# Splitting the sixth weight group of each expert, and the second gated half, in a hybrid attention and mixture-of-experts layer

## The chip, the cores and the metric

The kernel runs on one core of a Trainium2 chip, in one launch. The metric is the device time of one execution in microseconds (us), the median of several runs. A change of 1% is about 10 us here.

## The reference, cut to what matters

The layer is an attention and pooling block followed by a mixture of experts. Only the experts are touched by the change:

```
u: (1024 tokens, 1024)            16 experts, w_gate, w_up: 1024x512, w_down: 512x1024
top-1 group of 4, then top-2 experts inside it, softmax weights -> combine
for e in range(16):
    h = silu(u @ w_gate[e]) * (u @ w_up[e])
    y += combine[:, e] * (h @ w_down[e])
out = layer_norm(alpha * x + (1 + gate2) * y)
```

All arrays are fp32.

## The kernel before, in words

The first half of the kernel (attention, pooling, output projection, first layer norm, routing) ends a little after 540 us. From there the experts are worked through one after the other, unrolled in the program as `expert(0)` to `expert(15)`, and a final layer norm over all tokens closes the kernel.

Routing has sorted the tokens by expert. Each expert has a main block of 128 token slots, and a tail of up to 32 or 64 further tokens, which is run only where the expert has more than 128 (or 160) tokens, inside `tc.If(n_e > P)` (lines 1223 and 1242). With these inputs six experts run a tail, three of them a second one. From the third expert on, busy and less busy experts alternate.

The weights of an expert are six groups of 1 MB, `raw(0)` to `raw(5)`, each 128 partitions by 4 x 512 fp32. Groups 0 to 3 are gate and up, groups 4 and 5 are down. A ring of 11 buffers (`RAW`) holds them; SyncE's queue loads them far ahead (`refill`, `load_group`).

A product of the main block is made in one of two ways.
- Split (`mm_split`, lines 1056 to 1061): the weights are cut into a rounded high part in `HR`, copied by ScalarE (line 941), and the remainder in `LR`, subtracted by VectorE (line 944). The activations are cut the same way. Three matmuls in fp32r (a 4-byte format) then replace one fp32 product: high by high, high by low, low by high. A group is split in two halves of 128 x 1024 each (`split_group`). There are three buffers each for `HR` and `LR` (`NH = 3`), so a group's split waits until TensorE has finished with the group three places earlier; `split_ahead(s)` issues that split right behind the matmuls on group s.
- Plain fp32 (line 1176): TensorE takes the raw weights.

`NSP = 5` groups of an expert are split: the four of gate and up, and the first of down. The main block of one expert runs in this order: `gate_up(0)` (24 matmuls, columns 0 to 255 of gate and of up), `gated` (a0: Silu on ScalarE, the product on VectorE), `gate_up(1)` with `turn(a0)` inside it (two transposes of a0 on TensorE, then a copy out of PSUM; for a0 also the split, lines 1157 and 1158, into a tile `hs`), `gated` (a1), the tail's first half if there is one, `prep(e + 1)` (transposes and split of the next expert's tokens), `turn(a1)` (line 1161, a plain copy into `hh`), `down(0)` (12 split matmuls on group 4), `split_ahead`, `down(1)` (4 plain fp32 products on group 5), `emit` (two VectorE instructions out of PSUM, line 1195), `send` (an indirect DMA that adds the rows to `ybuf`), and the tail's second half.

The framework lays out the order on each engine itself, from the dependencies and its own estimate of when things are ready; each engine then works strictly in that order. In the trace the tail's second half (line 1242) lies in the middle of `down(0)`, and a0's transposes lie behind the 37th of the 48 matmuls of gate and up.

In the last expert the final layer norm of all tokens (`final`, lines 1002 to 1021) is threaded in: `tick()` counts the products and pulls one piece of it every second one. Its first instruction in a piece is ordered behind the newest ScalarE or VectorE instruction of the main path that `note` has recorded (`behind`).

Of the kernel before, what the change touches and what calls it, by code (L numbers as in the profile page):

```python
# [52 lines left out]
WS = "vvvv"  # L53
PRE = 0
SPLIT = 800
NSP = 5
RB = 0
TB = 1
MT = 2
# [33 lines left out]
def hybrid_layer(ctx: ExitStack, tc: tile.TileContext, x, c, w_ada, b_ada, w_qk, w_v, w_p, w_pool,  # L93
# [838 lines left out]
    def note(k, ins):  # L932
        newest[k] = ins
        return ins

    def split_group(s):
        m = NG * (s // NSP) + s % NSP
        r, l, h = RAW[m % NL], LR[s % NH], HR[s % NH]
        for a in range(2):
            cs = slice(2 * a, 2 * a + 2)  # L940
            rnd = note("a", nc.scalar.activation(h[:, cs], r[:, cs], AF.Copy))  # L941
            if s == 0:
                after(turned[0], rnd)
            sub = note("d", nc.vector.tensor_sub(l[:, cs], r[:, cs], h[:, cs]))  # L944
            if s < NH:
                after(ready, sub)
# [93 lines left out]
    def expert(e, n_e):  # L1040
# [10 lines left out]
        hts = []  # L1051

        def raw(g, j):
            return RAW[(NG * e + g) % NL][:, j]

        def mm_split(o, xh, xl, s, j, first, end):
            tick()
            h, l = HR[s % NH][:, j], LR[s % NH][:, j]
            nc.tensor.matmul(o, xh, h, start=first, stop=False)  # L1059
            nc.tensor.matmul(o, xh, l, start=False, stop=False)  # L1060
            nc.tensor.matmul(o, xl, h, start=False, stop=end)  # L1061

        def split_ahead(s):
            if s + NH < NE * NSP:
                split_group(s + NH)
# [22 lines left out]
        def tick():  # L1088
            ticks[0] += 1
            n = ticks[0] - BS1  # L1090
            if last and n >= 0 and n % BR1 == 0:
                next(bulk, None)

        def gate_up(half, mid=None):
            pg = ps.tile([P, 512], F32, name="mm", bufs=6)
            for k in range(KC):
                s = NSP * e + 2 * half + k // GRP
                mm_split(pg, xa_h[:, k], xa_l[:, k], s, k % GRP, k == 0, k == KC - 1)
# [52 lines left out]
        def turn(s):  # L1151
            pt = ps.tile([P, 2, P], F32, name="tr")
            for j in range(2):
                nc.tensor.transpose(pt[:, j], s[:, j * P:(j + 1) * P], ident)
            if not hts:
                hh = act.tile([P, 2, 2, P], F32R, name="hs")
                note("a", nc.scalar.activation(hh[:, 0], pt, AF.Copy))
                note("d", nc.vector.tensor_sub(hh[:, 1], pt, hh[:, 0]))
            else:
                hh = act.tile([P, 2, P], F32, name="hh", bufs=4)  # L1160
                note("a", nc.scalar.activation(hh, pt, AF.Copy))
            hts.append(hh)
# [3 lines left out]
        def down(g):  # L1166
            for dh in range(2):
                if g == 0:
                    pys.append(ps.tile([P, 512], F32, name="mm", bufs=6))
                for f in range(2):  # L1170
                    k, w = 2 * g + f, raw(4 + g, 2 * f + dh)
                    if g < NSP - 4:
                        mm_split(pys[dh], hts[g][:, 0, f], hts[g][:, 1, f], NSP * e + 4 + g, 2 * f + dh, k == 0, k == 3)
                    else:
                        tick()
                        nc.tensor.matmul(pys[dh], hts[g][:, f], w, start=k == 0, stop=k == 3)
# [41 lines left out]
        pa0 = gate_up(0)  # L1218
        a0 = gated(pa0)
        pa1 = gate_up(1, {MT: lambda: turn(a0)})  # L1220
        a1 = gated(pa1)
        t = {}
# [8 lines left out]
        if not last:  # L1231
            prep(e + 1)
        turn(a1)
        down(0)
        split_ahead(NSP * e + 4)
        down(1)
        ys_[1] = ytail
        for _ in bulk if last else ():
            pass
# [24 lines left out]
    for e in range(NE):  # L1264
        src = cnt[0:1, e:e + 1] if e < NS else cntp[0:1, e - NS:e - NS + 1]
        n_e = nc.values_load(src, min_val=0, max_val=S)
        if e == 0:
            scratch = act.tile([P, D], F32, name="y", bufs=1)[0:1, :2 * ND * ND].rearrange("p (r a b) -> p r a b", r=2, a=ND)
            for r, (o, v) in enumerate(((perm, eidx[0:1, NS:]), (cntp, cntf[:, NS:]))):
                calc = by_place(o, v, scratch[:, r])  # L1270
                after(ready, next(calc))
                next(calc, None)
        expert(e, n_e)
# [45 lines left out]
    with tc.If(top > P + HB):  # L1319
# [8 lines left out]
        e = nc.values_load(perm[0:1, ND - 1:ND], min_val=0, max_val=NE - 1)  # L1328
# [63 lines left out]
```

## Time and profile before

| | |
|---|---|
| Median of 3 runs | 1014.16 us (1008.32 to 1016.25) |
| Profiled execution, its own time | 1010.06 us |
| Its span, first to last instruction | 1008.3 us |
| Mean granted TensorE clock | 0.928 |
| Busy: TensorE, VectorE, ScalarE, GpSimd | 84%, 66%, 48%, 38% of the span |

The profile calls TensorE's matmuls PE and its weight loads PEld, VectorE DVE, ScalarE ACT, GpSimd POOL and SyncE's DMA queue SP. Times in a timeline count from the start of the span. The busy shares are means over stages with different limits; what the change is worth is read from the experts' stretch, about 557 to 957 us.

### The profile page before, as it was taken

How to read it: one execution, taken by the hardware profiler on the slowest of the kernel's cores; microseconds unless marked ns; L12 is line 12 of the kernel's file. 1: busy time of each engine (PE TensorE's matmuls, PEld its weight loads, DVE VectorE, ACT ScalarE, POOL GpSimd, SP SyncE). 2: the span in 40 equal slices, each digit the busy share in tenths (PEclk: the TensorE clock that was granted, in tenths of full speed). 3: DMA queues.
4: the chain of work that ended last, by engine and by line, in shares of the span. 5: the costliest groups of instructions: out<-in, count | busy, mean ns of one | idle time of the engine just before them, and what ended most of it. 6: DMA issues, size and time to landing. Idle time of an engine off the chain costs nothing. (4 is left out here: it accounts for less than half of the span.)

```text
span 1008.3 us, 14528 instructions
## 1 busy us (share of the span) xinstructions
PE 849.4 (84%) x4983; PEld 611.6 (61%) x4984; DVE 661.5 (66%) x990; ACT 487.3 (48%) x794; POOL 380.9 (38%) x337
## 2 busy tenths in 40 slices
PE   4979897999999888989882889999999999998820
PEld 3658675777767666766651666665666666666500
DVE  7889787374355656868486765657666575757553
ACT  3341453554454655444423555546555565656450
POOL 4685082060041335664554421212222222222383
PEclk7899998999999998988995989999999999999965
DMA  8937741010010342112647487778787888888731
GB/s 306 316 133 226 257 143 59 22 43 25 27 40 1 110 162 84 64 63 85 230 131 284 157 306 251 247 282 272 292 304 288 296 294 293 291 295 300 253 136 64
DMA packets 42488, 187.24 MB, mean 186 GB/s; under 512 B 7921, under 2 KB 8977, under 8 KB 30096
## 3 DMA queue, kind: packets, MB, share of 16 engines
q1 hardware_dynamic: 34608, 168.57, 45.5%
q0 software_dynamic: 7776, 17.33, 7.0%
q8 instruction: 61, 1.00, 0.4%
q14 instruction: 43, 0.35, 0.1%
HBM read 169.19 MB, written 25.33 MB: 193 GB/s over the span
## 5 line engine op out<-in xcount | busy, mean ns | idle before, releaser
L376 DVE TENSOR_TENSOR_SCAN N<-N,zcol 128x1023 f32<-128x1023 f32 (+7 forms) x64 | 88.9, 1426 | 86.5 <-ACT N L369 86.5
L1059 PE MATMUL mm<-HR,xa 128*128 128x512 f32 x256 | 106.6, 416 | 0.1
L1060 PE MATMUL mm<-LR,xa 128*128 128x512 f32 x256 | 101.3, 396 | 0.0
L961 POOL DMA_INDIRECT V<-u2d,TP x28 | 35.0, 1250 | 172.8 <-PEq L1223 65.5
L944 DVE TENSOR_TENSOR LR<-raw,HR 128x1024 fp32r<-128x1024 f32 x70 | 85.2, 1223 | 22.9 <-ACT HR L941 19.1
L1061 PE MATMUL mm<-HR,xa 128*128 128x512 f32 x256 | 99.8, 391 | 0.0
L941 ACT ACTIVATE HR<-raw 128x1024 fp32r<-128x1024 f32 x70 | 74.0, 1060 | 41.1 <-PE mm L1061 40.6
L944 DVE TENSOR_TENSOR LR<-mixT,HR 128x1024 fp32r<-128x1024 f32 x62 | 75.5, 1223 | 19.9 <-ACT HR L941 16.7
L941 ACT ACTIVATE HR<-mixT 128x1024 fp32r<-128x1024 f32 x62 | 65.3, 1058 | 37.4 <-PE mm L1061 37.3
L392 ACT ACTIVATE AT<-tr 128x512 f32<-128x512 f32 (+3 forms) x96 | 42.6, 487 | 51.6 <-PE tr L391 51.5
L446 PE MATMUL mm<-uh,wh 128*128 128x512 f32 x160 | 66.5, 416 | 0.2 <-ACT mixT L436 0.2
L448 PE MATMUL mm<-uh,wl 128*128 128x512 f32 x160 | 64.7, 404 | 0.0
L447 PE MATMUL mm<-ul,wh 128*128 128x512 f32 x160 | 64.5, 403 | 0.0
L419 POOL TENSOR_TENSOR mixT<-pT 128x344 f32<-128x344 f32 (+1 forms) x12 | 16.3, 1367 | 127.7 <-ACT pT L407 127.7
L391 PE MATMUL tr<-ident,arena 128*128 128x128 f32 x288 | 46.4, 299 | 18.0 <-ACT AT L392 9.2
L396 PE MATMUL mm<-AT,V 128*64 128x128 f32 x576 | 55.1, 302 | 3.9 <-ACT AT L392 3.1
L1059 PEld LDWEIGHTS mm<-HR,xa 128*128 128x128 f32 x256 | 48.3, 189 | 13.9 <-issue 4.1
L1060 PEld LDWEIGHTS mm<-LR,xa 128*128 128x128 f32 x256 | 48.4, 189 | 12.7 <-issue 3.6
L1061 PEld LDWEIGHTS mm<-HR,xa 128*128 128x128 f32 x256 | 48.1, 188 | 9.7
L391 PEld LDWEIGHTS tr<-ident,arena 128*128 128x128 f32 x288 | 36.8, 155 | 27.9 <-ACT AT L392 13.7
L378 DVE TENSOR_TENSOR arena<-arena,N 128x1023 f32<-128x1023 f32 (+7 forms) x64 | 53.6, 869 | 0.0
L649 PE MATMUL mm<-wol,mh 128*128 128x512 f32 x128 | 51.4, 401 | 2.2 <-POOL wol L533 1.7
(352 smaller groups left out, 2100.5 us busy)
## 6 DMA issues: line engine op xcount, KB each, us to landing
raw<-in_w_moe_dram SPq DMA_DIRECT2D x42, 1024.0 KB, 9.1
mixT<-in_w_moe_dram SPq DMA_DIRECT2D x36, 1024.0 KB, 10.1
arena<-in_w_moe_dram SPq DMA_DIRECT2D x18, 1024.0 KB, 9.8
arena<-in_w_ada_dram SPq DMA_DIRECT2D x24, 512.0 KB, 4.4
wada<-in_w_ada_dram SPq DMA_DIRECT2D x12, 512.0 KB, 6.1
mixT<-in_w_ada_dram SPq DMA_DIRECT2D x12, 512.0 KB, 4.1
ybuf<-sg SPq DMA_DIRECT2D x8, 512.0 KB, 2.6
wraw<-in_w_qk_dram SPq DMA_DIRECT2D x6, 512.0 KB, 3.4
```

Of the source, the lines that this page charges most:

```text
L376: nc.vector.tensor_tensor_scan(N[:, hd, 1:nk], N[:, hd, 1:nk], zcol.to_broadcast([P, nk - 1]), 1.0, op0=OP.mult, op1=OP.add)
L378: nc.vector.tensor_mul(E[:, hd, 1:nk], E[:, hd, 1:nk], N[:, hd, 1:nk])
L391: nc.tensor.transpose(pt[:, j], E[:, hd, (g + j) * P:(g + j + 1) * P], ident)
L396: mm = nc.tensor.matmul(po[h * HD:(h + 1) * HD, :P], V[:, cp, i + j, h * HD:(h + 1) * HD], ATs[h][j // 4][:, j % 4], start=j == 0, stop=j ...
L446: nc.tensor.matmul(po, h[:, k], uh[:, k, cs], start=k == 0, stop=False)
L447: nc.tensor.matmul(po, h[:, k], ul[:, k, cs], start=False, stop=False)
L448: nc.tensor.matmul(po, l[:, k], uh[:, k, cs], start=False, stop=k == KC - 1)
L941: rnd = note("a", nc.scalar.activation(h[:, cs], r[:, cs], AF.Copy))
L944: sub = note("d", nc.vector.tensor_sub(l[:, cs], r[:, cs], h[:, cs]))
L1059: nc.tensor.matmul(o, xh, h, start=first, stop=False)
L1060: nc.tensor.matmul(o, xh, l, start=False, stop=False)
L1061: nc.tensor.matmul(o, xl, h, start=False, stop=end)
```

## The change

`NSP` goes from 5 to 6, so that group 5 (the second of down) is split like the others, and `down(1)` uses `mm_split` instead of the plain product. `turn(a1)` makes the same split tile as `turn(a0)`. A `split_ahead` is added behind `down(1)`. The number of split buffers stays at three.

```
-NSP = 5
+NSP = 6
...
-            if not hts:
+            if len(hts) < NSP - 4:
                 hh = act.tile([P, 2, 2, P], F32R, name="hs")
                 note("a", nc.scalar.activation(hh[:, 0], pt, AF.Copy))
                 note("d", nc.vector.tensor_sub(hh[:, 1], pt, hh[:, 0]))
...
         split_ahead(NSP * e + 4)
         down(1)
+        split_ahead(NSP * e + 5)
         ys_[1] = ytail
```

## Rows read from the trace of the kernel before

**Rows 1.** The page: busy us, share of the span and instructions of each engine.
```profile
PE 849.4 (84%) x4983; PEld 611.6 (61%) x4984; DVE 661.5 (66%) x990; ACT 487.3 (48%) x794; POOL 380.9 (38%) x337
```
**Rows 2.** Windows: PE, PEld, DVE, ACT, POOL busy (instructions), clock, DMA share, GB/s.
```profile
817.00:846.00 29.00, 26.46 (x187) 17.66 (x186) 15.71 (x18) 15.75 (x24) 3.73 (x4) 1.00 0.82 303
846.00:866.50 20.50, 19.11 (x81) 13.67 (x80) 17.43 (x20) 12.90 (x16) 8.58 (x5) 1.00 0.82 279
```
**Rows 3.** Waits of the experts' stretch: total us, times, longest.
```profile
ACT HR L941 <- PE mm L1061: 87.5, 115, 5.2
```
**Rows 4.** Groups by shape from 440 us on: busy us, mean ns, idle before, releaser.
```profile
L1059 PE MATMUL mm<-HR,xa 128*128 128x512 f32 x256 | 106.6, 416 | 0.1
L944 DVE TENSOR_TENSOR LR<-raw,HR 128x1024 fp32r<-128x1024 f32 x70 | 85.2, 1223 | 22.9 <-ACT HR L941 19.1 <-DVEq L1223 0.2
...
L941 ACT ACTIVATE HR<-raw 128x1024 fp32r<-128x1024 f32 x70 | 74.0, 1060 | 41.1 <-PE mm L1061 40.6 <-ACTq L1223 0.2
...
L1176 PE MATMUL mm<-raw,hh 128*128 128x512 f32 x56 | 27.1, 628 | 0.0
...
L1158 DVE TENSOR_TENSOR hs<-tr,hs 128x256 fp32r<-128x256 f32 x16 | 6.7, 419 | 1.0 <-ACT hs L1157 1.0
...
L981 ACT ACTIVATE xb<-tr 128x256 f32<-128x256 f32 x12 | 3.9, 381 | 1.4 <-PE tr L980 1.4
```
**Rows 5.** Timeline of PE, end of an expert with one tail, and the next.
```profile
843.04 3.59 PE L1176 MATMUL mm<-raw,hh 128*128 128x512 f32 x8
...
846.71 0.39 PE L1060 MATMUL mm<-LR,xa 128*128 128x512 f32 x1
...
851.73 0.39 PE L1061 MATMUL mm<-HR,xa 128*128 128x512 f32 x1
...
854.91 0.39 PE L1154 MATMUL tr<-ident,silu 128*128 128x128 f32 x2
```
**Rows 6.** Timeline of DVE over the same stretch.
```profile
843.88 1.21 DVE L1137 TENSOR_TENSOR ytail<-ytail,sg 32x1024 f32<-32x1024 f32 x1 [6.20 <-ACT ytail L1136]
845.02 2.34 DVE L944 TENSOR_TENSOR LR<-mixT,HR 128x1024 fp32r<-128x1024 f32 x2
847.29 1.39 DVE L1195 SCALAR_TENSOR_TENSOR y<-mm,TP,sg 128x512 f32<-128x512 f32 x2
849.15 1.23 DVE L944 TENSOR_TENSOR LR<-mixT,HR 128x1024 fp32r<-128x1024 f32 x1 [0.47 <-ACT HR L941]
...
854.40 0.41 DVE L1148 TENSOR_TENSOR silu<-silu,mm 128x256 f32<-128x256 f32 x1
```
**Rows 7.** Timeline of DVE, end of the expert without a tail that follows.
```profile
863.75 2.36 DVE L944 TENSOR_TENSOR LR<-raw,HR 128x1024 fp32r<-128x1024 f32 x2 [1.72 <-ACT HR L941]
...
869.66 1.23 DVE L944 TENSOR_TENSOR LR<-raw,HR 128x1024 fp32r<-128x1024 f32 x1 [1.73 <-ACT HR L941]
```
**Rows 8.** Timeline of DVE, first subtraction of an expert behind two tails.
```profile
799.82 1.23 DVE L944 TENSOR_TENSOR LR<-mixT,HR 128x1024 fp32r<-128x1024 f32 x1 [0.22 <-ACT HR L941]
```
**Rows 9.** Timeline of PE: its waits at the tail's branch in two experts.
```profile
594.41 1.94 PE L971 MATMUL tr<-ident,V 128*128 128x128 f32 x8 [3.73 <-PEq L1223]
...
859.08 0.47 PE L1059 MATMUL mm<-HR,hs 128*128 128x512 f32 x1 [1.24 <-PEq L1223]
```
**Rows 10.** Windows around that longer wait, columns as in rows 2.
```profile
592.00:596.00 4.00, 1.59 (x8) 1.62 (x9) 1.35 (x2) 0.51 (x2) 1.00 (x1) 0.60 0.23 49
```
**Rows 11.** Timeline of DVE, then POOL, in the last expert and the final norm.
```profile
948.92 1.53 DVE L998 BATCH_NORM_STATS2 bn<-raw 128x6 f32<-128x512 f32 x2 [1.66 <-DMA raw<-ybuf]
...
953.79 1.29 DVE L998 BATCH_NORM_STATS2 bn<-raw 128x6 f32<-128x512 f32 x2 [3.09 <-DMA raw<-ybuf]
...
982.98 0.74 DVE L1195 SCALAR_TENSOR_TENSOR y<-mm,TP,sg 128x512 f32<-128x512 f32 x1
...
955.61 0.83 POOL L1008 TENSOR_SCALAR mod<-mod 128x1 f32<-128x1 f32 x1 [1.18 <-DVE mod L1000]
```

More of the change, by code (lines that the diff above doesn't have):

```diff
@@ L55 @@
 SPLIT = 800
-NSP = 5
+NSP = 6
 RB = 0
@@ L1154, in turn @@
                 nc.tensor.transpose(pt[:, j], s[:, j * P:(j + 1) * P], ident)
-            if not hts:
+            if len(hts) < NSP - 4:
                 hh = act.tile([P, 2, 2, P], F32R, name="hs")
@@ L1236, in expert @@
         down(1)
+        split_ahead(NSP * e + 5)
         ys_[1] = ytail
```

## The prediction

> **What bounds the kernel now.** The page comes first [rows 1]: TensorE is busy 84% of the span, VectorE 66%. The change lies in the experts alone, so the next view is the windows of one pair of experts, one with a tail and the one without that follows it [rows 2]. In both TensorE is busy over 90% of the time at the full clock of 2.4 GHz (granted 1.00), but VectorE is not the same in the two: 15.71 of 29.00 us with a tail, 17.43 of 20.50 us without. The waits [rows 3] say who leads: ScalarE's rounding copies waited 87.5 us for TensorE to give a split buffer back, and no DMA stands there, so the weights land in time and TensorE sets the pace. The timelines of the pair [rows 5 to 7] then show how far behind TensorE the other two are when each piece is wanted, and the last expert's timeline [rows 11] which part of the end hangs on what.
>
> **What TensorE saves.** The four plain products of `down(1)` are eight records. They start at 843.04; the next expert's second matmul starts at 846.71, and its first took one step before that. A step is read from the split matmuls: 22 of them from 846.71 to 851.73 make 0.228 us each [rows 5]. So plain fp32 holds TensorE for 846.71 - 0.228 - 843.04 = 3.44 us, and the twelve split matmuls will hold it for 12 x 0.228 = 2.74 us: 0.70 us less per expert. I take the step between starts, not the durations, which overlap. The Trainium skill, in "Perfetto Trace Analysis", section "Identifying the Most-Contended Engine", says that matmul busy time is no measure, because matmuls are pipelined. By the durations [rows 4] the eight records would cost 8 x 0.628 = 5.02 us and the twelve 12 x 0.416 = 4.99 us, and the saving would be nothing; the trace sides with the rule, since twelve durations of 0.416 us do not fit into the time between starts.
>
> The saving counts in experts 0 to 14: 15 x 0.70 = 10.5 us. In the last expert it does not: its own rows leave PSUM at 982.98 [rows 11], behind the final norm's work on VectorE, long after its matmuls.
>
> **What it adds.** Per expert two ScalarE copies of 1.06 us, two subtractions of 1.22 us, and the low half of a1, 0.42 us, on VectorE [rows 4]. Two subtractions in a row take 2.34 us [rows 6], which is the figure used below.
> - ScalarE: the new copies stand behind the last matmuls of `down(1)`. ScalarE does 12.90 us of work in 20.50 [rows 2] and waits there for TensorE; 15.0 in 19.8 still fits. Nothing.
> - a1's low half: VectorE waits 1.72 us just there in an expert without a tail [rows 7], 6.20 us with one [rows 6]. Nothing; without that cover 0.42 us.
> - SyncE: group 5's buffer now comes free when it has been split, during `gate_up(1)`, and not behind `down(1)`. The loads queued behind it go out earlier. Since no wait is for weights [rows 3], nothing. The splits of the next expert's groups 0, 1 and 2 each move one group later. The tightest is group 2: its subtractions would be done at 851.0 (below), and TensorE asks for it 24 steps, 5.47 us, after its start at 845.78, at 851.25; the second half is asked for later still. In time, with little left.
> - VectorE's extra pair behind an expert without a tail: 2.34 us of work and a start that comes 0.70 us earlier, against 1.73 us of idle time [rows 7], leaves it 1.3 us late; the y instructions ahead of it wait for `down(1)` and so also move by up to 0.7, which leaves 0.6. From there to a0's multiply the four subtractions come at TensorE's pace, 854.40 - 849.15 = 5.25 us, where they could take 2 x 2.34 = 4.68 [rows 6]: 0.57 us is made up. Nothing is left; at most 0.7 us in each of nine such experts, 6.3 us.
> - VectorE's extra pair behind a tail. Here the queue is fuller: the tail's own multiply at 843.88, the pair for the next expert, the two y instructions up to 847.29 + 1.39 = 848.68 [rows 6]. With the new pair behind them VectorE is free at 848.68 + 2.34 = 851.02. TensorE's next expert starts at 843.04 + 2.74 = 845.78 and not 846.48, so the first subtraction of that expert, now 849.15 - 846.48 = 2.67 us behind the start, is wanted at 848.45. VectorE is 2.57 us late; 0.57 is made up, and a0's multiply comes 2.0 us late. And a0's multiply has no slack: it ends at 854.40 + 0.41 = 854.81 [rows 6], and a0's transposes start at 854.91 [rows 5], in the middle of TensorE's stream, with the next matmuls queued behind them in order. Behind two tails VectorE's idle time was 0.22 and not 0.47 us [rows 6, 8], so 2.25 us late. Six experts have a tail, since the copies of line 981 come twice in each and there are twelve [rows 4].
>
> The price of this last point is open between 0 and 3 x 2.0 + 3 x 2.25 = 12.75 us. Nothing, if the new order on TensorE puts later work where it would wait; all of it, if the order stays. The order is laid out anew for the changed program, and transposes that start 0.10 us behind the multiply's end look like an order that counts VectorE's time. Then they move back, and VectorE meets TensorE again at a1's multiply, another four subtractions and 0.57 us later: 2.0 - 0.57 = 1.4 us late, in a chain (multiply, transposes, copy, subtraction, `down(1)`) that has only `down(0)`'s 2.74 us to hide behind and hid there exactly before. I take 1.4 us, six times: 8.4 us.
>
> **The end.** The final norm starts from the landing of expert 14's rows, so it moves with TensorE's sum. In the last expert one more pair is subtracted, ahead of the norm's first statistics at 948.92, which waited 1.66 us for a DMA [rows 11]; that covers it. The second statistics at 953.79 were free of the main path. Now the newest recorded VectorE instruction there is a1's low half, behind Silu, multiply, transposes and copy, and the statistics are ordered behind it. GpSimd waits for them at 955.61 and is busy from then on. Estimate from these rows: a1's low half at about 955.3, so 1.5 us late; between 0 and 1.6. I take 1.5, as GpSimd's wait is plain.
>
> Sum: -10.5 + 8.4 + 1.5 = -0.6 us. On the profiled execution's 1010.06 us that gives 1009.5. It lies 4.1 us under the median of the runs; on the median the forecast is 1013.5 us, no measurable change. Its own range is -6 to +5 us, for a stall of 0.5 to 2.2 us behind a tail.
>
> **The rivals.**
> - VectorE's lateness is hidden and the whole saving arrives. For it: VectorE has 13 us to spare in an expert with a tail [rows 2], so what is late must only be carried there, by an order that puts a0's and a1's transposes far enough back. Against it: the chain of a1 has little to hide behind. 1014.16 - 10.5 = 1003.7 us.
> - Slower: the stalls cost TensorE its clock. In the trace TensorE once waited 3.73 us at a branch [rows 9], and the granted clock of the window around it fell to 0.60 [rows 10], between its two levels of 1.2 and 2.4 GHz; a wait of 1.24 us [rows 9] left it at 1.00 [rows 2]. The new stalls of 2.0 to 2.25 us lie between. From wherever between those two waits the clock falls, each costs another 40% of 4 us, 1.6 us. With the order unchanged: -10.5 + 12.75 + 1.5 + 6 x 1.6 = +13.4 us, 1027.5 us. Against it: matmuls stand close on both sides of each stall.
> - The change does not act as written: the new order moves the tail's branch or the evacuations elsewhere, and the time moves for reasons outside this sum, by a few us either way. The 3.73 us wait, whose cause the rows do not show, could go or come again.
>
> **How the numbers follow.** 0.55 for the forecast, 0.25 for the hidden lateness, 0.12 for the clock, 0.08 for the rest. 1% is about what a measurement of this kernel tells from no change. Faster by more than that needs all of the saving and something more, or an end without its 1.5 us: 0.18. Slower by more: the clock, and the upper end of the costs (12.75 + 6.3 + 1.6 - 10.5 = +10.2): 0.15. Within 1%: 0.67. The range takes in the hidden case and the upper end of the costs, 1002.5 to 1023 us, and leaves out the clock.
>
> **What would show it.** Starts of one expert's `down(1)` and of the next expert 2.74 us apart, 0.70 less than before. VectorE without idle time from the tail's multiply through the first subtractions of the next expert. A new wait of TensorE on VectorE at line 1154, at a0 or a1, in the six experts that follow a tail, and none in the others. Granted clock 1.00 there. If no such wait stands there, the lateness was hidden; if TensorE waits for a subtraction of line 944 instead, group 2 came too late, and the price is larger than I set it.

## The result, and the profile after

The changed kernel takes 1039.63 us (median of 4 runs, 1038.15 to 1041.72), the kernel before 1011.88 us on the same chip (4 runs, 1008.32 to 1016.25): 1.0274 times as long, 95% interval 1.0224 to 1.0324. That is slower by 2.7%, and outside the predicted range. The profiled execution took 1041.72 us, its span is 1039.9 us.

The page's first line, as in [rows 1], shows more of the same work and no engine that became the bound:

```profile
PE 852.0 (82%) x5047; PEld 630.9 (61%) x5048; DVE 697.1 (67%) x1038; ACT 518.9 (50%) x826; POOL 446.1 (43%) x337
```

Where the time went is read from the starts of the experts (the first split matmul of each). From the first start to that of the last expert it is 379.7 us in the trace before, 409.9 after: 30.2 of the 31.6 us by which the span grew arise among the experts. Windows over just these stretches, first the trace before, then after (columns as in [rows 2]):

```profile
557.46:937.18 379.72, 350.81 (x2131) 241.62 (x2131) 251.91 (x280) 218.87 (x308) 96.01 (x72) 0.98 0.79 279
```
```profile
557.30:967.20 409.90, 352.71 (x2191) 258.85 (x2191) 282.92 (x323) 246.71 (x337) 161.47 (x72) 0.96 0.72 259
```

TensorE's busy time grew by 1.9 us, its idle time from 28.9 to 57.2 us: it waits. GpSimd is busy 65 us longer with the same 72 instructions, and the clock is granted at 0.96 instead of 0.98. The waits say what TensorE waits for, and what VectorE waits for (total, times, longest). The first line, TensorE at a0's transposes, and the second, VectorE at the landing of y, are not there at all among the experts before; the third answers to [rows 3], and over the same stretch, up to the start of the last expert, it was 83.1 us before: ScalarE waits less for TensorE, which leads by less.

```profile
PE tr L1154 <- DVE silu L1148: 25.8, 11, 3.0
```
```profile
DVE y L1195 <- DMA ybuf<-y,TP: 14.0, 4, 4.2
...
ACT HR L941 <- PE mm L1061: 64.2, 101, 5.4
```

The pair of experts of [rows 2], 28.85 and 20.50 us before, starts at 833.73, 866.15 and 888.74 after; the third window is the next expert with a tail:

```profile
833.73:866.15 32.42, 27.17 (x191) 19.37 (x190) 17.39 (x21) 17.47 (x27) 5.79 (x4) 0.95 0.77 284
866.15:888.74 22.59, 18.92 (x85) 14.37 (x84) 20.06 (x23) 15.06 (x19) 16.85 (x4) 1.00 0.71 255
888.74:920.47 31.73, 26.12 (x191) 18.24 (x190) 17.16 (x21) 17.47 (x27) 5.92 (x4) 1.00 0.79 285
```

Both kinds of experts are slower. VectorE's timeline behind the tail, the counterpart of [rows 6]:

```profile
865.12 1.22 DVE L1137 TENSOR_TENSOR ytail<-ytail,sg 32x1024 f32<-32x1024 f32 x1 [5.87 <-ACT ytail L1136]
866.26 2.34 DVE L944 TENSOR_TENSOR LR<-arena,HR 128x1024 fp32r<-128x1024 f32 x2
868.53 0.73 DVE L1195 SCALAR_TENSOR_TENSOR y<-mm,TP,sg 128x512 f32<-128x512 f32 x1
869.19 2.34 DVE L944 TENSOR_TENSOR LR<-mixT,HR 128x1024 fp32r<-128x1024 f32 x2
871.46 0.73 DVE L1195 SCALAR_TENSOR_TENSOR y<-mm,TP,sg 128x512 f32<-128x512 f32 x1
872.12 4.61 DVE L944 TENSOR_TENSOR LR<-mixT,HR 128x1024 fp32r<-128x1024 f32 x4
876.66 0.40 DVE L1148 TENSOR_TENSOR silu<-silu,mm 128x256 f32<-128x256 f32 x1
876.99 1.21 DVE L944 TENSOR_TENSOR LR<-mixT,HR 128x1024 fp32r<-128x1024 f32 x1
```

No brackets behind the first line: VectorE never idles from the tail's multiply to a0's. Between the two stand four pairs of subtractions instead of three, and TensorE, which has to have a0's product for its transposes, stands still (its timeline, counterpart of [rows 5]):

```profile
874.76 0.39 PE L1061 MATMUL mm<-HR,xa 128*128 128x512 f32 x1
877.12 0.44 PE L1154 MATMUL tr<-ident,silu 128*128 128x128 f32 x2 [1.97 <-DVE silu L1148]
```

Now GpSimd behind a tail, first the trace before, then after; then VectorE and TensorE in the expert after it. Here is what the prediction had not looked at:

```profile
845.88 2.85 POOL L1205 DMA_INDIRECT ybuf<-ytail,TP  x1 [7.87 <-ACT HR L941]
```
```profile
867.11 12.44 POOL L1205 DMA_INDIRECT ybuf<-ytail,TP  x1 [8.32 <-ACT HR L941]
879.86 2.39 POOL L1205 DMA_INDIRECT ybuf<-y,TP  x1 [0.30 <-PEq L1223]
```
```profile
892.94 0.75 DVE L1195 SCALAR_TENSOR_TENSOR y<-mm,TP,sg 128x512 f32<-128x512 f32 x1 [4.04 <-DMA ybuf<-y,TP]
893.61 2.39 DVE L944 TENSOR_TENSOR LR<-raw,HR 128x1024 fp32r<-128x1024 f32 x2
895.93 0.74 DVE L1195 SCALAR_TENSOR_TENSOR y<-mm,TP,sg 128x512 f32<-128x512 f32 x1
896.59 4.61 DVE L944 TENSOR_TENSOR LR<-raw,HR 128x1024 fp32r<-128x1024 f32 x4
901.13 0.40 DVE L1148 TENSOR_TENSOR silu<-silu,mm 128x256 f32<-128x256 f32 x1
```
```profile
901.59 0.44 PE L1154 MATMUL tr<-ident,silu 128*128 128x128 f32 x2 [3.00 <-DVE silu L1148]
```

The scatter of the tail's rows (the indirect DMA of `send`) keeps GpSimd for 12.44 us, against 2.85 in the trace before. The scatter of y stands behind it in GpSimd's queue: y was complete at 872.2, its scatter begins at 879.86. `y` has one buffer, so the next expert's y instruction, whose turn was at 888.90, waits until 892.94 for that transfer to land; behind it in VectorE's queue stand the pairs and the next a0, and TensorE waits again, 3.00 us, in an expert that has no tail ahead of it.

Both scatters of a tail end in step with VectorE. The one of the trace before ends 1.37 us behind the end of the pair of subtractions at 847.36 [rows 6], the held one 1.35 us behind the end of the subtraction at 878.20. So it is everywhere: in the fourteen traces, those of the experiments included, all 79 scatters of a tail's rows that took over 2.5 us end 1.35 to 1.37 us behind the end of a subtraction of line 944. What sets the length is which subtraction that is; in the held one eight others ended between its start and that one.

### The profile page after: what moved, and what is told of

Its sections match the earlier page's. It is cut to its first block, busy times and chain, and to the rows that moved or that the text cites. A ratio compares the mean times of both kernels' runs of the same rounds, so it can differ in the third digit from the quotient of the medians.

```text
span 1039.9 us, 14782 instructions
## 1 busy us (share of the span) xinstructions
PE 852.0 (82%) x5047; PEld 630.9 (61%) x5048; DVE 697.1 (67%) x1038; ACT 518.9 (50%) x826; POOL 446.1 (43%) x337
## 5 line engine op out<-in xcount | busy, mean ns | idle before, releaser
L1205 POOL DMA_INDIRECT ybuf<-ytail,TP x13 | 76.6, 5894 | 110.0 <-ACT HR L941 83.2
L1059 PE MATMUL mm<-HR,xa 128*128 128x512 f32 x256 | 105.4, 412 | 4.3 <-PEq L1223 4.1
L944 DVE TENSOR_TENSOR LR<-raw,HR 128x1024 fp32r<-128x1024 f32 x84 | 99.2, 1216 | 9.7 <-ACT HR L941 9.5
L1060 PE MATMUL mm<-LR,xa 128*128 128x512 f32 x256 | 103.9, 406 | 0.4 <-DVE LR L944 0.4
L1061 PE MATMUL mm<-HR,xa 128*128 128x512 f32 x256 | 103.3, 404 | 0.0
L941 ACT ACTIVATE HR<-raw 128x1024 fp32r<-128x1024 f32 x84 | 87.7, 1058 | 27.6 <-PE mm L1061 26.0
L944 DVE TENSOR_TENSOR LR<-mixT,HR 128x1024 fp32r<-128x1024 f32 x72 | 85.3, 1214 | 14.7 <-ACT HR L941 13.2
L941 ACT ACTIVATE HR<-mixT 128x1024 fp32r<-128x1024 f32 x72 | 74.9, 1056 | 29.3 <-PE mm L1061 27.8
L961 POOL DMA_INDIRECT V<-u2d,TP x28 | 31.0, 1106 | 108.0 <-issue 51.2
L1059 PE MATMUL mm<-HR,hs 128*128 128x512 f32 x128 | 54.9, 429 | 8.7 <-ACT hs L1157 2.6
L1059 PEld LDWEIGHTS mm<-HR,xa 128*128 128x128 f32 x256 | 50.6, 198 | 15.5 <-issue 5.1
L1061 PEld LDWEIGHTS mm<-HR,xa 128*128 128x128 f32 x256 | 50.3, 196 | 10.7
```

Source lines behind the costliest of these rows:

```text
L1205: sc = nc.gpsimd.indirect_dma_start(out=out if last else ybuf[:], out_offset=bass.IndirectOffsetOnAxis(ap=slots(e, b, n)[0], axis=0), in_= ...
```

## The experiments

Durations are those of the same two neighbours in each trace, expert 10 (one tail) and expert 11 (none); "tail scatter" is how long GpSimd is busy with the scatter of a tail's rows; "a0" and "y" are the total waits of TensorE for a0's multiply and of VectorE for the landing of y, up to the start of the last expert. For the scatter the table gives the length in most of the six tails. The ratio is to the kernel before, timed on the same chip (medians 1008.4, 1008.9 and 1009.4 us in the three groups of runs). The changed kernel was timed beside a kernel before of 1011.88 us; where a difference to it is given, it is one of medians, and by the ratios it comes out 1 to 3 us smaller.

| run | median us | ratio, 95% interval | exp. 10, 11 | tail scatter | a0 | y |
|---|---|---|---|---|---|---|
| before | 1008.4 to 1009.4 | | 28.85, 20.50 | 2.85 | 0 | 0 |
| after | 1039.63 | 1.0274 (1.0224-1.0324) | 32.43, 22.59 | 12.44 | 25.8 | 14.0 |
| products_only | 1003.0 | 0.9934 (0.9906-0.9962) | 27.68, 20.85 | 2.85 | 1.3 | 3.7 |
| no_low5 | 1025.55 | 1.0152 (1.0104-1.0201) | 27.79, 24.24 | 11.0 | 14.8 | 3.6 |
| y2 | 1017.36 | 1.0084 (1.0049-1.0119) | 27.72, 22.62 | 12.44 | 12.4 | 0 |
| mt6 | 1059.2 | 1.0491 (1.0445-1.0537) | 33.29, 23.98 | 16.2 | 9.1 | 35.8 |
| late_splits | 1008.05 | 0.9984 (0.9958-1.0009) | 28.17, 22.16 | 2.85 | 0 | 0 |
| late_ring | 1021.66 | 1.0101 (1.0067-1.0136) | 28.16, 22.61 | 5.1 | 7.6 | 0 |
| gap | 1020.48 | 1.0098 (1.0064-1.0131) | 28.24, 22.15 | 2.85 | 1.6 | 0 |
| act_busy | 1021.26 | 1.0102 (1.0063-1.0142) | 27.70, 23.20 | 4.64 | 0 | 0 |
| mul_first | 1028.6 | 1.0195 (1.0143-1.0246) | 28.21, 21.34 | 2.85 | 4.6 | 15.1 |
| mul_first_y2 | 1012.56 | 1.0036 (1.0013-1.0060) | 28.20, 21.24 | 2.85 | 2.1 | 0 |
| no_low5_y2 | 1019.55 | 1.0078 (1.0055-1.0102) | 27.72, 22.59 | 11.0 | 11.9 | 0 |
| y2_before | 1007.59 | 0.9982 (0.9950-1.0014) | 28.82, 20.57 | 2.85 | 0 | 0 |

**TensorE's part alone (products_only).** The kernel before with `down(1)` in split products; they read the buffers of the next expert's group 0, so the right weights of group 5 are left out.

```diff
-            if not hts:
+            if True:
...
-                    if g < NSP - 4:
+                    if True:
```

> Five groups are split as before the change; a1 is split too, and down(1) makes twelve split products, but reads the split buffers of the next expert's first group, so the right weights of group 5 are left out and no further split is made. All theories that blame VectorE's extra pair expect the whole saving of 0.70 us per expert and no stall at line 1154: about 1001 us (1011.9 - 10.5), a little more if the norm's second statistics come late. If twelve split products don't save what I read from the steps, it stays at 1010 to 1013.

5.4 us faster by the medians. The saving is real: an expert with one tail takes 27.68 instead of 28.85 us. The next gives back 0.35; TensorE waits there 0.16 us for a0's multiply and 0.52 us for VectorE's work on the next expert's tokens, waits that expert 11 does not have in the trace before.

**VectorE's part of the split taken out (no_low5).** The changed kernel, without the two subtractions of each group 5.

```diff
+            if s % NSP == 5:
+                continue
             sub = note("d", nc.vector.tensor_sub(l[:, cs], r[:, cs], h[:, cs]))
```

> The changed kernel, but the low part of group 5 is not subtracted (the products with it read what the buffer held before; that part of the result is left out). ScalarE's two copies and all matmuls stay. If VectorE's extra pair is the cause, by whatever path, it falls to about 1001 to 1005 us, GpSimd's scatters take 1.5 to 2.9 us again and no transposes at line 1154 wait. If ScalarE's copies, the later splits of the next expert's groups, or the new order on the engines are the cause, it stays above 1030.

Neither of the two times expected. VectorE has its old amount of work, and the kernel is still 1.5% slower than before: seven a0 waits, 14.8 us, stay, and the scatter still takes 11.0 us. So the sum of VectorE's work is not the whole cause. What stays is the place: behind a tail there are still the pairs of two groups of the next expert. But the kernel is 14.1 us faster than the changed one (1039.63 - 1025.55): the waits for y fall from four to one, and of the five a0 waits in experts without a tail ahead of them one is left. With one buffer for y the added work does cost.

**A second buffer for y (y2), also in the kernel before (y2_before).**

```diff
-            y = ys_[0] = act.tile([P, D], F32, name="y", bufs=1)
+            y = ys_[0] = act.tile([P, D], F32, name="y", bufs=2)
```

> The changed kernel with two buffers for y in place of one. Theory A: VectorE without gaps holds GpSimd's scatter of the tail's rows up (12.4 us), y's scatter behind it goes late, and y's only buffer then holds VectorE, and through it a0's multiply, in the expert after. Then the stalls behind a tail stay (six of about 2.3 us) and those in the five experts one further on go (3.2, 2.6, 3.4, 3.4, 2.9 us), with some of the half-clock windows: 1020 to 1026 us. Theory B, VectorE is late by its own work alone: no change, 1037 to 1041.

> The kernel before with two buffers for y, nothing else: there the y scatter goes out within 3 us behind the tail's, and no wait of VectorE for the y tile shows. Both theories: no difference, 1005 to 1011 us. It says what a second y buffer is worth by itself; were it over 5 us faster, the gain of the second buffer in the changed kernel would not be the change's doing.

In the changed kernel it takes away 22.3 us; in the kernel before it changes nothing that can be measured. The scatter stays as long as it was, but nobody waits for y, and up to the last expert the a0 waits are left only in the six experts behind a tail. GpSimd, then TensorE's wait, of y2:

```profile
855.44 12.44 POOL L1205 DMA_INDIRECT ybuf<-ytail,TP  x1 [8.32 <-ACT HR L941]
868.19 2.38 POOL L1205 DMA_INDIRECT ybuf<-y,TP  x1 [0.30 <-PEq L1223]
```
```profile
PE tr L1154 <- DVE silu L1148: 12.4, 6, 2.2
```

This parts the loss in two. From products_only to y2 it is 1017.36 - 1003.0 = 14.4 us, of which these waits are 12.4; from y2 to the changed kernel it is the 22.3 us that the one buffer of y costs with all that follows from it. The traces agree: from the first expert's start to the last's it is 379.7 us in before, 371.9 in products_only, 387.2 in y2 and 409.9 in after, so 7.8 us saved, then 15.3 and 22.7 lost.

**a0's transposes later (mt6).** The changed kernel with a0's transposes issued behind the seventh instead of the third step of the second half.

```diff
-MT = 2
+MT = 6
```

> The changed kernel with a0's transposes put in four products later (MT 6 for 2). If the stall is only the place of the transposes in TensorE's order, both kinds of stall shrink by four products of 0.68 us, so to nothing: 1005 to 1015 us. If VectorE is the limit, the wait only moves to a1's transposes or to down(0): 1030 to 1040.

A miss, in the wrong direction. The transposes did move, from 39 to 45 matmuls behind the expert's start, and the a0 waits fall to 9.1 us; but TensorE now waits for line 944, the scatter takes 16.2 us, and VectorE's waits for y grow to 35.8 us. Waits of TensorE, then of VectorE, of mt6:

```profile
PE mm L1060 <- DVE LR L944: 18.5, 6, 5.3
```
```profile
DVE y L1195 <- DMA ybuf<-y,TP: 35.8, 5, 9.6
```

**The place of the splits (late_splits, late_ring).** Both are the kernel before, with its work unchanged and the next expert's groups split one group later in the program.

```diff
-                if k % GRP == GRP - 1:
-                    split_ahead(s)
+                if k % GRP == GRP - 1 and (half, k // GRP) != (1, 0):
+                    split_ahead(s - half)
...
-        split_ahead(NSP * e + 4)
+        split_ahead(NSP * e + 3)
         down(1)
+        split_ahead(NSP * e + 4)
```

> The kernel before (five groups split, plain fp32 products for the last group, the same work on every engine) with one thing of the change alone: the next expert's groups 0, 1 and 2 are split one group later, so that the pairs of two groups instead of one stand behind a tail on VectorE. Theory A (the place of the splits costs, not their number): VectorE comes some 2.3 us late to the next expert's first gated multiply, TensorE waits there as in the changed kernel, the scatter of a tail's rows is held for about 10 us, and a later expert waits for the y tile: 12 to 25 us over the kernel before, 1020 to 1033 us, the lower end because a plain down(1) gives VectorE 0.7 us more per expert. Rival B (the sixth group's split, work added to VectorE and ScalarE, costs): no difference from the kernel before, 1005 to 1011 us, tail-less experts 20.5 us as before.

No difference (expert 11 has a wait of 2.28 us at its tail's branch in this trace; experts 5, 7, 9 and 13 take 21.04 to 21.08 us). The trace says why: VectorE's order behind a tail was that of the kernel before, one pair and then the y instructions. The program's order alone does not set it; the framework's planner moved the split ahead again, presumably because its buffer was free. So late_ring also takes the buffers as six groups on three take them, and keeps group 2 behind group 1:

```diff
-        r, l, h = RAW[m % NL], LR[s % NH], HR[s % NH]
+        r, l, h = RAW[m % NL], LR[s % NSP % NH], HR[s % NSP % NH]
...
+            if s >= NH and s % NSP == 2:
+                after(order[-1], rnd)
+            order.append(rnd)
```

> The kernel before (five groups split, the same work on every engine) with the order that six groups force on the three split buffers: the next expert's group 1 takes the buffer of the current group 4 and so can only be split behind down(0), and group 2 is split behind it, so that two pairs instead of one stand behind a tail (the run late_splits had not reached that, its order on VectorE was that of the kernel before). Theory A (what costs is the further pair that the buffers push behind a tail): VectorE reaches the multiply of a0 2.3 us late in the experts behind a tail, the tail's scatter is held, 12 to 25 us over the kernel before, 1020 to 1033 us. Rival B (VectorE's total work, the sixth pair, costs): 1005 to 1011 us, no difference.

12.3 us slower than the kernel before, with the same instructions and the same data; the a0 waits are 7.6 of them. VectorE behind a tail (the two y instructions now behind both pairs), and TensorE's waits, in late_ring:

```profile
853.79 2.34 DVE L949 TENSOR_TENSOR LR<-arena,HR 128x1024 fp32r<-128x1024 f32 x2
856.06 2.34 DVE L949 TENSOR_TENSOR LR<-mixT,HR 128x1024 fp32r<-128x1024 f32 x2
858.33 1.39 DVE L1200 SCALAR_TENSOR_TENSOR y<-mm,TP,sg 128x512 f32<-128x512 f32 x2
859.65 4.61 DVE L949 TENSOR_TENSOR LR<-mixT,HR 128x1024 fp32r<-128x1024 f32 x4
864.19 0.40 DVE L1153 TENSOR_TENSOR silu<-silu,mm 128x256 f32<-128x256 f32 x1
```
```profile
PE tr L1159 <- DVE silu L1153: 7.6, 6, 1.5
```

Expert 11 takes 22.61 us, as in y2. **no_low5_y2** asks the same from the other side, with VectorE's old amount of work and the buffers of six groups:

> The changed kernel without VectorE's subtractions for an expert's group 5 (the low part of that group is left out, as in no_low5) and with two buffers for y: VectorE's work is that of the kernel before, the order behind a tail still that of six groups. Theory A (two pairs behind a tail cost, not the total of VectorE's work): the a0 waits behind tails stay at 2 to 2.6 us, seven of them, and the time is that of the changed kernel with two y buffers, 1012 to 1020 us. Rival B (total work): 996 to 1004 us, the full saving of 0.70 us per expert.

1019.55 us and 11.9 us of a0 waits, in the six experts behind a tail: nothing is gained over y2 by taking the sixth pair away. With two buffers for y it is the place that costs, not the amount.

**What holds the scatter (gap, act_busy).** gap adds two waits to the changed kernel, so that VectorE idles shortly behind a tail:

```diff
+            if s >= NH and (s % NSP, a) in ((2, 1), (3, 0)):
+                after(subs[-1], rnd, mybir.DependencyClass.Sync)
```

> The changed kernel with two waits added: the rounding copy of the second half of the next expert's group 2, and that of the first half of the group behind it, wait for VectorE's subtraction just before, so VectorE idles for 0.5 to 1.3 us at two places behind a tail; all work stays. Theory A (the tail's scatter on GpSimd is held as long as VectorE runs subtractions without a break): the scatter ends in one of these gaps, in 3 to 6 us instead of 12.4, the y scatter follows at once, the waits of VectorE for the y tile vanish (some 14 us and the stalls behind them), and in spite of some 1 to 2 us of added lateness behind each tail the kernel gets faster, 1022 to 1035 us. Rival B (the scatter is held by something else, the transfer of the rows itself or the loads): it stays at 11 to 12.5 us, and the added lateness makes the kernel slower than the changed one, 1045 to 1060 us.

With two waits more the kernel is 19.1 us faster than the changed one; the wait for y is gone. Not all of that is the scatter: the planner also moved a0's transposes, from 39 to 41 matmuls behind the expert's start, so the a0 waits fall to 1.6 us, and TensorE waits 6.7 us for the subtractions (line 948 here) instead. And the row is not the one expected: the scatter ends at 857.48, ahead of VectorE's first idle time at 858.57, 1.36 us behind the end of the pair at 856.12. GpSimd, VectorE and ScalarE of gap:

```profile
854.63 2.85 POOL L1210 DMA_INDIRECT ybuf<-ytail,TP  x1 [8.12 <-ACT HR L943]
```
```profile
853.78 2.34 DVE L948 TENSOR_TENSOR LR<-arena,HR 128x1024 fp32r<-128x1024 f32 x2
856.05 0.73 DVE L1200 SCALAR_TENSOR_TENSOR y<-mm,TP,sg 128x512 f32<-128x512 f32 x1
856.71 1.20 DVE L948 TENSOR_TENSOR LR<-mixT,HR 128x1024 fp32r<-128x1024 f32 x1
857.84 0.73 DVE L1200 SCALAR_TENSOR_TENSOR y<-mm,TP,sg 128x512 f32<-128x512 f32 x1
```
```profile
858.29 3.91 ACT L943 ACTIVATE HR<-mixT 128x1024 fp32r<-128x1024 f32 x4 [2.84 <-DVE LR L948]
```

Up to there VectorE ran what it runs in the changed kernel, at the same distances (pair, y at +2.27 us, subtraction at +2.93). What differs in these rows is ScalarE, idle for 2.84 us. So act_busy fills that idle time with two copies that nobody reads:

```diff
+            if s >= NH and (s % NSP, a) == (2, 1):
+                spare = act.tile([P, 1024], F32, name="spare", bufs=1)
+                for _ in range(2):
+                    after(rnd, nc.scalar.activation(spare, r[:, cs].rearrange("p c n -> p (c n)"), AF.Copy))
```

> As the run gap, but ScalarE, which idled 2.8 us there while it waited for VectorE, copies one half group twice more into a tile that nobody reads (the only work added). Behind a tail VectorE's instructions are the same in the run gap and in the changed kernel for the 2.8 us in which the scatter ended in the one and did not in the other; ScalarE's were not. Theory A (VectorE's run of subtractions holds GpSimd's scatter, ScalarE has no part): the tail's scatters stay at 2.8 to 3.3 us. Rival B (the scatter needs a stretch in which ScalarE is idle as well): they are held again, 5 to 12.5 us. Time 1018 to 1026 us by A, 1030 to 1045 us by B.

```profile
803.08 4.64 POOL L1214 DMA_INDIRECT ybuf<-ytail,TP  x1 [10.85 <-ACT HR L947]
```
```profile
805.17 1.20 DVE L952 TENSOR_TENSOR LR<-arena,HR 128x1024 fp32r<-128x1024 f32 x1
```
```profile
802.86 2.13 ACT L946 ACTIVATE spare<-arena 128x1024 f32<-128x1024 f32 x2
806.46 1.06 ACT L947 ACTIVATE HR<-arena 128x1024 fp32r<-128x1024 f32 x1 [1.46 <-DVE LR L952]
```

Between the two: the scatter takes 4.64 us behind four of the tails (3.0 behind two) and the time is that of gap. The rows above are GpSimd, VectorE and ScalarE of act_busy: the scatter now ends 1.35 us behind the end of this subtraction at 806.37, one subtraction later than in gap. So ScalarE's copies have a part, by these rows, in which subtraction's end lets the scatter go on, but they alone do not hold it for 12 us.

**a0's multiply ahead of the split of group 4 (mul_first, mul_first_y2).** In the changed kernel the pair of group 4 stands ahead of a0's multiply in VectorE's queue, though nobody needs it yet.

```diff
         a0 = gated(pa0)
+        split_ahead(NSP * e + 1, (newest["a"], newest["d"]))
```

> The changed kernel, with the split of an expert's group 4 issued behind the first half's gated Silu and multiply instead of ahead of them; all work stays. Theory A (a0's multiply, queued behind subtractions that nobody needs yet, is what TensorE waits for): the 2.3 to 3.4 us waits ahead of a0's transposes, 25.8 us in all, fall below 5 us, and the half-clock stretches behind them too: 1003 to 1018 us, the upper end if the tail's scatter is still held and the y tile still waits. Rival B (VectorE has too much to do behind a tail, whatever its order): the wait moves to the groups whose splits are now later, TensorE waiting at line 944's subtractions, and the time stays at 1030 to 1042 us.

> As the one with the multiply ahead of group 4's split, with two buffers for y. Theory A (the two causes, the late multiply behind a tail and the one y buffer, are all that the change lost): both stalls gone, the saving of 0.70 us per expert shows, tail-less experts 19.8 to 20.2 us, 996 to 1004 us, the best of all. Rival B (VectorE has too much to do): 1012 to 1020 us, as with two y buffers alone.

Between both theories: the a0 waits fall from 25.8 to 4.6 us, but VectorE still waits 15.1 us for y in two places, behind the two tails whose scatters take 10.5 and 13.9 us (2.85 behind the other four); with two y buffers 1012.56 us are left, 4.8 less than y2 and above the 996 to 1004 expected. With them expert 11 falls from the 22.62 us of y2 to 21.24, not to 19.8: the transposes of line 1158 now wait 10.4 us in all, 14 times, for VectorE's work on the next expert's tokens (3.6 us in y2). By these waits the lateness moved to the next place where TensorE needs VectorE. No version here that computes all of the reference is measurably faster than the kernel before.

## Why the prediction was wrong

The forecast was -0.6 us, the measured change +27.75 us by the medians. Two steps failed: the stall behind a tail was sized too small, on the word of one sentence about the planner, and GpSimd's scatter with y's one buffer stood at nothing, without a reason. The second is the larger.

**TensorE's saving, 10.5 us: the mechanism right, the sum too large.** The step that the prediction named as a sign came, in expert 11 after; the first row begins `down(1)`, the second the next expert:

```profile
885.95 0.39 PE L1059 MATMUL mm<-HR,hs 128*128 128x512 f32 x1
...
888.74 0.39 PE L1059 MATMUL mm<-HR,xa 128*128 128x512 f32 x1
```

That is 2.79 us against 3.44 before, 0.65 us less per expert. Alone (products_only) the saving brought 5.4 us by the medians, 3.8 to 9.5 by its interval, and 7.8 us among the experts of its trace: part of it goes to waits for VectorE, as in expert 11 above.

**ScalarE's copies, a1's low half, SyncE's loads, the extra pair behind an expert without a tail, at nothing: in part shown.** With two buffers for y the extra pair costs nothing measurable by its amount (no_low5_y2 against y2), and in y2 the a0 waits stand behind tails alone; with one buffer its subtractions cost 14.1 us (no_low5), by the wait for y. For line 944 TensorE waits 0.4 us once in the changed kernel: group 2 comes in time. ScalarE's copies and a1's low half were in no run taken out alone, so that they cost nothing is not shown.

**The pair behind a tail, 1.4 us six times: the mechanism right, the size wrong.** VectorE without a gap from the tail's multiply on, and the new wait at line 1154 on a0, are as forecast; the wait is 1.97 us at 877.12, and in y2, where nobody waits for y, 12.4 us in six experts: not the 8.4 taken but the 12.75 named as the upper end. Two terms were off. First, I let TensorE start its next expert 0.70 us earlier. These are the first matmul behind the tail, before, and then after with the next expert's start:

```profile
841.77 0.50 PE L1060 MATMUL mm<-LR,hs 128*128 128x512 f32 x1
```
```profile
863.01 0.50 PE L1061 MATMUL mm<-HR,hs 128*128 128x512 f32 x1
...
866.15 0.39 PE L1059 MATMUL mm<-HR,xa 128*128 128x512 f32 x1
```

After, the next expert starts 3.14 us behind it, before it was 4.71 us (to 846.48, the start that the prediction works out from steps): 1.57 us earlier, because the new order puts all but the last step of `down(0)` ahead of the tail. Second, I argued that the planner would move a0's transposes back out of the wait. It moved them from 37 to 39 matmuls behind the expert's start, 0.45 us, which does not cover even the further 0.87 us. The sentence that failed is "Then they move back, and VectorE meets TensorE again at a1's multiply"; the other branch, "all of it, if the order stays", was the right one. late_ring shows this mechanism by itself, in the kernel before: 12.3 us slower, with 7.6 us of a0 waits.

**What no step had: the scatter and the one buffer of y, 22.3 us.** The prediction followed VectorE's lateness to TensorE alone and asked of no other engine what a gapless VectorE does to it. The row was on the page (GpSimd's scatters), and `bufs=1` in the code. It shows twice: y2 removes the waiting party and gets 22.3 us back; gap shortens the holding and gets 19.1 back, by adding waits, in part through the later transposes. The stalls in experts that have no tail ahead of them, which my list of signs said would not be there, come from this.

A rule that bears on it could have been read. The Trainium skill, in "SBUF — State Buffer", section "Who interferes with whom", says that a VectorE instruction with two SBUF inputs contends with a GpSimd instruction that reads SBUF, and that whichever is issued first blocks the other until it ends. The same section of the Trainium skill says that a `tensor_tensor` did not stall a DMA in a probe, so the Trainium skill alone does not settle whether this scatter falls under the rule. Line 944 is such an instruction with two SBUF inputs, and the traces agree in kind: the held scatters end at a fixed 1.35 to 1.37 us behind the end of a subtraction. In size they don't: by the rule the scatter would have gone on when the subtraction under way ended, and here eight ended before the one behind which it went on. The same section of the Trainium skill says that ScalarE never waits on anyone, and it gives ScalarE no port that the two share, while in act_busy two ScalarE copies, with VectorE's rows unchanged up to there, moved the scatter from 2.85 to 4.64 us. Which subtraction's end lets the scatter go on stays open.

**The clock, my slower rival: partly true.** The granted clock fell behind some of the stalls and not behind others of the same length: 0.52 behind the wait of 3.01 us at 845.88, 1.00 behind that of 3.00 us at 901.59.

```profile
845.60:849.00 3.40, 3.12 (x9) 2.55 (x10) 2.94 (x5) 1.44 (x2) 0.00 (x0) 0.52 0.85 217
```
```profile
901.60:905.00 3.40, 3.14 (x19) 2.35 (x19) 3.40 (x4) 2.31 (x3) 0.00 (x0) 1.00 0.60 122
```

Nine records of TensorE's matmuls fall in the one stretch, nineteen in the other. Five such stretches stand in the trace after that have no counterpart before, and two in y2's; by an estimate from the window above, half of 3.4 us, they cost up to 1.7 us each. They are within the parts above, not beside them, since they follow the stalls.

**The end, +1.5 us:** from the last expert's start it is 71.1 us before and 72.7 after. The number agrees, but it is not shown, since no run takes the step out: with the work of the kernel before the same stretch is 70.3 us in late_splits and 67.8 in y2_before, whose second y buffer serves the final norm too.

**The range.** Its upper end of 1023 us should take in the upper end of the costs; on the median those give 1014.16 + 10.2 = 1024.4 us. The measured 1039.63 us lies beyond both, so this slip decided nothing.

## What to carry to other kernels

When an edit closes the gaps of an engine, look not only at who waits for its results but at who works in those gaps: here it was GpSimd's scatter, and the bill came an expert later, through a tile with one buffer. Where n groups go through a ring of m buffers, the ring and not the program text decides which work lands behind a branch; count, for the new n, which buffer is free there. And when a forecast rests on a planner covering a lateness, take the uncovered price as the forecast and the covered one as the hope.

## What the runs showed of the hardware

- A scatter that GpSimd issues (64 rows at most) took 1.48 us at its shortest in the trace after, 2.85 us in four of six tails of the kernel before, 12.44 us in five of six tails of the changed kernel, and 16.2 us in five of six in mt6. It is no slowdown in proportion: in fourteen traces all 79 that took over 2.5 us end 1.35 to 1.37 us behind the end of one of VectorE's 128x1024 subtractions.
- y's scatter (128 rows) can get through between such subtractions: in the trace after, VectorE runs four of them without a gap from 778.92 on, and the scatter from 779.28 to 781.57 takes 2.29 us, 1.44 us from the end of the first of them (780.13), against 1.57 us at its shortest there.
- Two added waits made a kernel 1.8% faster (1039.63 to 1020.48 us).
- The y scatter took longer from issue to landing, 11.8 us in the median against 8.9 us before, though in the experts' stretch 7% fewer bytes per second were moved (259 against 279 GB/s). Why is open.
